# PEER's second choice among 50 sums instead of 256

## The chip, the cores and the metric

The kernel runs on one core of a Trainium2 chip, written in the Tile framework, which puts the instructions of each engine into an order of its own and sets all semaphores. The metric is device time of the whole program in microseconds, as the median of several runs.

## The reference, cut to what matters

Two blocks of a network run over 512 tokens of width 1024: RWKV mixer, feed-forward, gated unit, feed-forward, attention, and at the end PEER, a layer of 16384 one-neuron experts. For each token and each of 8 heads PEER scores two lists of 128 keys, takes the best 16 of each list (first choice), forms all 256 sums of the two lists of sixteen, takes the best 16 of those (second choice), and looks up which pair of keys each winner stands for:

```python
s = jnp.einsum('thpd,hpnd->thpn', q, sub_keys).astype(jnp.float32)
sv, si = lax.top_k(s, PEER_TOPK)
cand = sv[:, :, 0, :, None] + sv[:, :, 1, None, :]
cidx = si[:, :, 0, :, None] * PEER_NKEYS + si[:, :, 1, None, :]
...
fv, fpos = lax.top_k(cand, PEER_TOPK)
eidx = jnp.take_along_axis(cidx, fpos, axis=-1).reshape(C, PEER_HEADS * PEER_TOPK)
g = jax.nn.softmax(fv, axis=-1).reshape(C, PEER_HEADS * PEER_TOPK)
u = u_tab[eidx]
a = jax.nn.gelu(jnp.einsum('ted,td->te', u, hb).astype(jnp.float32), approximate=False)
coef = (g * a).astype(hb.dtype)
vv = v_tab[eidx]
return jnp.einsum('te,ted->td', coef, vv)
```

Both lists come sorted, so a sum at position (a, b) has at least (a+1)(b+1)-1 sums that are no smaller; only pairs with (a+1)(b+1) up to 16 can win, and there are 50 of them.

## The kernel before, in words

The tokens lie in four tiles of 128. Tile 0 gathers its own experts: 256 rows of 1024 numbers are fetched by indirect DMA from GpSimd's queue (L1292) and multiplied on VectorE (L1304, L1308); generator `own`, advanced by `some`. Tiles 1 to 3 do it densely: for each block of 128 experts, an `act` (L1262) multiplies the expert table with all 384 tokens (24 matmuls of 384 columns in three parts; a weight split in two numbers, the high part on ScalarE L102, the low part on VectorE L103, or on GpSimd for every fifth block) and puts the activation into DRAM. 112 of the 128 blocks are computed ahead, as work that `fill` strews among the rest. For tiles 1 to 3 the chosen pairs are turned into weights on a grid of 128 by 128 keys: `onehots` (L1437) makes one-hot rows on VectorE (L1445, L1447, L1450), `grids` (L1453) multiplies them on TensorE (L1470), in 32 units a tile.

The order in which the program is written:

- a loop over 16 half-heads computes the scores; the first choice for tile 0 (`top`, five VectorE operations, L1337 to L1341: max, index of the eight, replace, max, index) stands in it, and an `act` after each fourth;
- `picks(0)`, the second choice and the lookup for tile 0, with `pace(FA, 0)` at each yield; its result `eu`, `ev` (L1435) starts the gathering;
- `tops(1)` to `tops(3)`, the first choice of the other tiles, with half an `act` and 0.3 of an own row a yield;
- `picks(1)`; then `picks(2)` with three units of `grids(1)` a yield, `picks(3)` with those of `grids(2)`, then `grids(3)`;
- `fill(NS)`, the rest of the 112 blocks, and then a loop over 128 blocks that weights the activations and multiplies with the second table; at its 127th step the own rows that are left are done, `some(256)`, and after the last one tile 0 is finished (L1578, L1579) and all are stored.

`picks` yields 14 times: one for each head, one after the softmax, one after the weights are turned, and two for each of two decodings. At each yield `pace` adds 0.2 of an `act` (FB, FA) and, for tiles 1 to 3, 0.2 of an own row (S1). The scheduler takes this order as a priority only: on each engine it picks, by its own estimate of when things are ready, the earliest written instruction that can go, so later work is pulled ahead where an engine would wait. Buffers limit that: the pool of `picks` has two of each tile, the weights three. On the chip each engine then runs its list strictly in order.

A decoding turns 128 positions (0 to 255) into key numbers. For the row a shift, for the column a mask (L1415, L1417); ScalarE widens the 128 numbers to 128 by 16 (L1420), VectorE compares them with 0 to 15 (L1421), multiplies with the sixteen key numbers (L1423) and adds the sixteen up in four steps (L1426, L1428). TensorE then transposes the result (L1399) and ScalarE copies it to `IT` or `JT`, from which `onehots` reads.

Of the kernel before, what the change touches and what calls it, by code (L numbers as in the profile page):

```python
# [9 lines left out]
F32 = mybir.dt.float32  # L10
F32R = mybir.dt.float32r
F16 = mybir.dt.float16
BF = mybir.dt.bfloat16
I32 = mybir.dt.int32
U32 = mybir.dt.uint32
AF = mybir.ActivationFunctionType
OP = mybir.AluOpType
# [23 lines left out]
class Kern:  # L41
# [1193 lines left out]
    def peer(self):  # L1235
        nc, tc, I = self.nc, self.tc, self.I
# [7 lines left out]
        with ExitStack() as cx:  # L1244
# [5 lines left out]
            pi = cy.enter_context(tc.tile_pool(name="pei", bufs=1))  # L1250
            iof = pi.tile([128, 128], F32, name="iof")
            IT, JT = [pi.tile([128, TD], F16, name=n) for n in ("IT", "JT")]
            WW = pi.tile([128, 2, TD], F16, name="WW")
            io4 = pi.tile([128, 128, 4], F16, name="io4")
            io16 = pi.tile([128, 16], F16, name="io16")
# [3 lines left out]
            nc.vector.tensor_copy(io4, iof[:, :, None].to_broadcast([128, 128, 4]))  # L1259
            nc.vector.tensor_copy(io16, iof[:, 0:16])  # L1260

            def act(j, gl=None):  # L1262
                w = self.wload(I["pe_u"][j], [128, 8, 128], eng=nc.gpsimd if j % WP == WP - 1 else None)
                bk = self.bank()[:, 0:TD]
                for k in range(8):
                    self.mm3(bk, (w[0][:, k, :], w[1][:, k, :]), (hT[0][:, k, 128:], hT[1][:, k, 128:]), k == 0, k == 7)
                if gl is None:
                    gl = pg.tile([128, TD], F32, name="gl")
                nc.scalar.activation(gl, bk, AF.Gelu)  # L1269
                return gl  # L1270
# [54 lines left out]
            for h in range(2):  # L1325
                bk = self.bank("x")
# [6 lines left out]
            sv = [pi.tile([128, 16, 16], F32, name=f"sv{t}") for t in range(NT)]  # L1333
            si = [pi.tile([128, 16, 16], U32, name=f"si{t}") for t in range(NT)]

            def top16(src, vals, idx, work):
                nc.vector.max(vals[:, 0:8], src)  # L1337
                nc.vector.max_index(idx[:, 0:8], vals[:, 0:8], src)
                nc.vector.match_replace(work, vals[:, 0:8], src, -3e38)  # L1339
                nc.vector.max(vals[:, 8:16], work)  # L1340
                nc.vector.max_index(idx[:, 8:16], vals[:, 8:16], work)  # L1341
# [8 lines left out]
            with tc.tile_pool(name="pe2", bufs=2) as q2:  # L1350
# [4 lines left out]
                for hp in range(16):  # L1355
# [3 lines left out]
                    bk = self.bank("x")  # L1359
# [15 lines left out]
            def picks(t):  # L1375

                q2 = q3
                fv = q2.tile([128, 8, 16], F32, name="fv")
                fp = q2.tile([128, 8, 16], U32, name="fp")
                for h in range(8):  # L1380
                    cand = q2.tile([128, 256], F32, name="cand")
                    nc.vector.tensor_tensor(cand.rearrange("p (a b) -> p a b", a=16),
                                            sv[t][:, 2 * h, :, None].to_broadcast([128, 16, 16]),
                                            sv[t][:, 2 * h + 1, None, :].to_broadcast([128, 16, 16]), op=OP.add)
                    wk = q2.tile([128, 256], F32, name="wk2")
                    top16(cand, fv[:, h, :], fp[:, h, :], wk)
                    yield
                wt = g0.rearrange("p (h k) -> p h k", h=8) if t == 0 else q2.tile([128, 8, 16], F32, name="wt")
                nc.vector.tensor_tensor(wt, fv, fv[:, :, 0:1].to_broadcast([128, 8, 16]), op=OP.subtract)
                nc.scalar.activation(wt, wt, AF.Exp)  # L1390
# [6 lines left out]
                def turn(src):  # L1397
                    bk = self.bank("x")
                    nc.tensor.transpose(bk[:, 0:128], src.rearrange("p h k -> p (h k)"), self.ident)  # L1399
                    return bk[:, 0:128]  # L1400
# [7 lines left out]
                yield  # L1408
                sif = q2.tile([128, 8, 2, 16], F16, name="sif")
                nc.vector.tensor_copy(sif, si[t].rearrange("p (h e) a -> p h e a", e=2))  # L1410
                ijs = []
                for e, dst in ((0, IT), (1, JT)):
                    ab = q2.tile([128, 8, 16], U32, name="ab")
                    if e == 0:
                        nc.vector.tensor_scalar(ab, fp, 4, None, op0=OP.logical_shift_right)  # L1415
                    else:
                        nc.vector.tensor_scalar(ab, fp, 15, None, op0=OP.bitwise_and)  # L1417
                    oh = q2.tile([128, 8, 16, 16], F16, name="oh")
                    ohr = oh.rearrange("p h k a -> p (h k) a")
                    nc.scalar.copy(ohr, ab.rearrange("p h k -> p (h k)")[:, :, None].to_broadcast([128, 128, 16]))  # L1420
                    nc.vector.tensor_tensor(ohr, ohr, io16[:, None, :].to_broadcast([128, 128, 16]), op=OP.is_equal)  # L1421
                    yield
                    nc.vector.tensor_mul(oh, oh, sif[:, :, e, None, :].to_broadcast([128, 8, 16, 16]))  # L1423

                    for n in (8, 4, 2):
                        nc.vector.tensor_add(ohr[:, :, 0:n], ohr[:, :, 0:n], ohr[:, :, n:2 * n])  # L1426
                    ij = q2.tile([128, 8, 16], F32, name="ij")
                    nc.vector.tensor_add(ij.rearrange("p h k -> p (h k)"), ohr[:, :, 0], ohr[:, :, 1])  # L1428
                    yield
                    if t:  # L1430
                        nc.scalar.copy(dst[:, ts], turn(ij))
                    ijs.append(ij.rearrange("p h k -> p (h k)"))
                if t == 0:
                    for dst, m, n in ((eu, ijs[0], ijs[1]), (ev, ijs[1], ijs[0])):
                        nc.vector.scalar_tensor_tensor(dst, m, 128.0, n, op0=OP.mult, op1=OP.add)  # L1435
# [246 lines left out]
```

## Time and profile before

| | us |
|---|---|
| median of 3 runs | 3099.87 (3099.35 to 3113.97) |
| profiled execution, its own time | 3095.69 |
| its span | 3093.9 |
| TensorE busy | 2951.7 (95%) |
| VectorE busy | 2091.1 (68%) |
| ScalarE busy | 1156.3 (37%) |
| GpSimd busy | 646.3 (21%) |
| mean granted TensorE clock | 0.971 |

The span is from the first instruction to the last; the execution's own time has 1.8 us more around it. Busy time says little by itself: matmuls overlap, so a busy TensorE is judged by how many it starts in a stretch. Operations of VectorE overlap too: the duration of a row is longer than the distance to the next row's start, and it is that distance that the engine's time goes by. PEER begins at about 1756 us and holds the last 43% of the span.

### The profile page before, as it was taken

What the parts mean: (1) busy time and instruction counts of PE and PEld (TensorE: products, weight loads), DVE (VectorE), ACT (ScalarE), POOL (GpSimd) and SP (SyncE); (2) the same over time, 40 slices, a digit from 0 to 9 for tenths busy, and PEclk for the clock granted to TensorE, in tenths of its full rate; (3) what the DMA queues carried; (4) which work ended last, traced back from release to release, by engine and by line L of the source; (5) the groups of instructions that cost most, each with busy time, mean ns of one, the idle gap of its engine ahead of it and who ended that gap; (6) DMA issues with size and microseconds to landing.
All of it is one profiled execution on the core that took longest, in us unless ns stands there. A gap on an engine that the chain in (4) does not pass through costs nothing.

```text
span 3093.9 us, 43610 instructions
## 1 busy us (share of the span) xinstructions
PE 2951.7 (95%) x16121; PEld 2483.1 (80%) x16121; DVE 2091.1 (68%) x4694; ACT 1156.3 (37%) x1918; POOL 646.3 (21%) x593
## 2 busy tenths in 40 slices
PE   7977899999999999999999999989999999999998
PEld 6755787888888788888875888989999888787887
DVE  7663775533247666425776678999988477888787
ACT  5533433322223332223565433344433333333332
POOL 1023221000000000000000003345444434444453
PEclk9978999999999999999998999999999999999999
DMA  4235654222324267533220234678888889999996
GB/s 143 92 85 192 162 144 130 93 91 95 95 89 143 76 214 234 164 95 92 77 85 2 68 101 161 227 244 294 282 292 287 294 307 322 336 341 321 327 335 223
DMA packets 217553, 569.03 MB, mean 184 GB/s; under 512 B 64474, under 2 KB 80090, under 8 KB 217212
## 3 DMA queue, kind: packets, MB, share of 16 engines
q1 hardware_dynamic: 144508, 362.71, 35.8%
q0 software_dynamic: 64096, 200.89, 19.1%
q10 hardware_dynamic: 8736, 2.65, 0.4%
q8 instruction: 126, 2.06, 0.3%
q14 instruction: 87, 0.71, 0.1%
HBM read 504.24 MB, written 61.87 MB: 183 GB/s over the span
## 4 chain that ended last, share of the span: by engine, by line
PE 75%; DVE 12%; DMA 6%; issue 4%; ACT 2%; POOL 1%; POOLq 0%; SPq 0%; DVEq 0%; ACTq 0%
PE b L276 19%; PE b L124 15%; PE b L123 15%; PE b L122 15%; PE b L1470 3%; DMA gl<-ga 2%; DVE wlo L103 2%; DVE er L1304 1%; PE b L1161 1%; PE b L959 1%; DVE hr L1308 1%; DMA er<-in_pe_ur,eu 1%; PE b L1179 1%; DVE wk L1339 1%; PE b L678 1%
## 5 line engine op out<-in xcount | busy, mean ns | idle before, releaser
L102 ACT CAST whi<-wst 128x1024 fp32r<-128x1024 f32 (+2 forms) x491 | 510.7, 1041 | 1165.4 <-PE b L123 436.1
L103 DVE TENSOR_TENSOR wlo<-wst,whi 128x1024 fp32r<-128x1024 f32 (+2 forms) x466 | 563.3, 1210 | 442.5 <-ACT whi L102 426.2
L124 PE MATMUL b<-hTh,wlo 128*128 128x384 f32 (+2 forms) x1992 | 716.4, 360 | 13.7 <-DVE wlo L103 13.4
L122 PE MATMUL b<-hTh,whi 128*128 128x384 f32 (+2 forms) x1992 | 722.4, 363 | 2.5 <-ACT hTh L223 1.5
L123 PE MATMUL b<-hTl,whi 128*128 128x384 f32 (+2 forms) x1992 | 717.0, 360 | 2.2 <-DVE hTl L224 2.2
L124 PEld LDWEIGHTS b<-hTh,wlo 128*128 128x128 f32 x1992 | 377.7, 190 | 57.0 <-DVE wlo L103 18.4
L122 PEld LDWEIGHTS b<-hTh,whi 128*128 128x128 f32 x1992 | 379.2, 191 | 42.3 <-ACT hTh L223 2.2
L123 PEld LDWEIGHTS b<-hTl,whi 128*128 128x128 f32 x1992 | 378.4, 190 | 40.9 <-DVE hTl L224 3.0
L122 PE MATMUL b<-whi,ch 128*128 128x512 f32 x768 | 304.7, 397 | 5.4 <-ACT ch L102 5.4
L124 PE MATMUL b<-whi,cl 128*128 128x512 f32 x768 | 304.6, 397 | 1.2 <-DVE cl L103 1.2
L123 PE MATMUL b<-wlo,ch 128*128 128x512 f32 x768 | 304.5, 396 | 0.3 <-DVE wlo L103 0.3
L1292 POOL DMA_INDIRECT er<-in_pe_v,ev x128 | 196.0, 1531 | 241.1 <-DVE hr L1308 216.1
L1292 POOL DMA_INDIRECT er<-in_pe_ur,eu x128 | 171.6, 1340 | 90.1 <-DVE er L1304 58.5
L122 PEld LDWEIGHTS b<-whi,ch 128*128 128x128 f32 x768 | 144.8, 189 | 39.8 <-ACT ch L102 5.7
L124 PEld LDWEIGHTS b<-whi,cl 128*128 128x128 f32 x768 | 144.6, 188 | 36.8 <-DVE cl L103 2.0
L123 PEld LDWEIGHTS b<-wlo,ch 128*128 128x128 f32 x768 | 144.8, 189 | 34.9 <-DVE wlo L103 0.7
L1308 DVE SCALAR_TENSOR_TENSOR hr<-er,a,hr 128x1024 f32<-128x1024 f32 x127 | 164.4, 1294 | 0.1
L1304 DVE SCALAR_TENSOR_TENSOR er<-er,hr 128x1024 f32<-128x1024 f32 x128 | 156.3, 1225 | 8.5 <-DMA er<-in_pe_ur,eu 8.5
L1274 POOL DMA_DIRECT2D ga<-gl x112 | 64.8, 579 | 345.1 <-ACT gl L1269 332.0
L276 PE MATMUL b<-whi,hTh 128*128 128x512 f32 (+2 forms) x336 | 129.3, 386 | 0.8 <-ACT P L971 0.8
L276 PE MATMUL b<-whi,hTl 128*128 128x512 f32 (+2 forms) x336 | 129.4, 385 | 0.4 <-DVE hTl L103 0.4
L276 PE MATMUL b<-wlo,hTh 128*128 128x512 f32 (+2 forms) x336 | 129.6, 386 | 0.0
(556 smaller groups left out, 4954.8 us busy)
## 6 DMA issues: line engine op xcount, KB each, us to landing
wst<-in_pe_u SPq DMA_DIRECT2D x128, 512.0 KB, 4.7
wst<-in_pe_v SPq DMA_DIRECT2D x128, 512.0 KB, 6.2
wst<-in_ffn_gu SPq DMA_DIRECT2D x88, 512.0 KB, 3.7
wst<-in_ad_w SPq DMA_DIRECT2D x48, 512.0 KB, 4.1
wst<-in_ffn_dn SPq DMA_DIRECT2D x44, 512.0 KB, 3.6
ga<-gl POOLq DMA_DIRECT2D x112, 192.0 KB, 4.2
gl<-ga SPq DMA_DIRECT2D x112, 192.0 KB, 5.0
gd<-G SPq DMA_DIRECT2D x40, 512.0 KB, 6.5
```

Source lines behind the costliest of these rows:

```text
L102: self.nc.scalar.copy(hi, src)
L103: (eng or self.nc.vector).tensor_sub(lo, src, hi)
L122: mm(out, a[0], b[0], start=start, stop=False)
L123: mm(out, a[0], b[1], start=False, stop=False)
L124: mm(out, a[1], b[0], start=False, stop=stop)
L276: self.nc.tensor.matmul(banks[t][:, :n], self.chunk(aT, a, k + kk)[:, t * 128:(t + 1) * 128], w[b][:, kk, :], start=seen[t] == 1, stop=see ...
L678: mm(bk[:, q * 256:(q + 1) * 256], BT[:, c, 2 * g + q, :], AT[:, c, 2 * g + q].rearrange("p e n -> p (e n)"), start=True, stop=True)
L1274: nc.gpsimd.dma_start(ga[j], act(j))
L1292: d = nc.gpsimd.indirect_dma_start(out=r, out_offset=None, in_=src, in_offset=bass.IndirectOffsetOnAxis(ap=idx[:, k:k + 1], axis=0))
L1304: d = nc.vector.scalar_tensor_tensor(r, r, 1.0, hr, op0=OP.mult, op1=OP.mult, accum_out=a0[:, k:k + 1])
L1308: d = nc.vector.scalar_tensor_tensor(y0, r, a0[:, k - 128:k - 127], y0, op0=OP.mult, op1=OP.add)
L1470: mm(bk[:, e * 128:(e + 1) * 128], oi[:, u % OT // 4, :, e], oj[:, w, u % OT // 4, :, e], start=(w == 0), stop=(w == 1))
```

## The change

The sums of all eight heads are formed at once, and only the 50 that can win: seven additions (rows a = 0, 1, 2, 3, 4 with 16, 8, 5, 4 and 3 sums each, rows 5 to 7 together with 2 each, rows 8 to 15 together with 1 each) replace eight of 256. So the second choice of any head stands behind the first choice of all heads. The five operations of the choice run on 50 elements; `picks` yields once after the sums, once for each two heads, once each after the softmax and the weights, and five times in the lookup: 12 times in place of 14.

A position 0 to 49 no longer holds row and column in its bits. The position is compared with the sixteen starts of the rows (`st16`): the result is 1 for each row up to the right one. Multiplied with the differences between neighbouring key numbers (`dsi`) and added up, that is the row's key number; multiplied with the row lengths (`dst16`) and added up, it is the row's start, which is taken from the position to give the column, and the column is decoded as before. So there are three sums over sixteen in place of two, and the second widening waits for the first. Two constants are made once, with 18 small fills on GpSimd.

```diff
--- before.py
+++ after.py
@@ -1259,6 +1259,18 @@
             nc.vector.tensor_copy(io4, iof[:, :, None].to_broadcast([128, 128, 4]))
             nc.vector.tensor_copy(io16, iof[:, 0:16])
 
+
+            NC = 50
+            seg = [16, 8, 5, 4, 3, 2, 2, 2] + [1] * 8
+            begin = [sum(seg[:a]) for a in range(16)]
+            st16, dst16 = [pi.tile([128, 16], F16, name=n) for n in ("st16", "dst16")]
+            nc.vector.tensor_scalar(st16, iof[:, 0:16], 34.0, None, op0=OP.add)
+            for a in range(8):
+                nc.gpsimd.memset(st16[:, a:a + 1], float(begin[a]))
+            nc.gpsimd.memset(dst16, 1.0)
+            for a in range(9):
+                nc.gpsimd.memset(dst16[:, a:a + 1], float(seg[a - 1]) if a else 0.0)
+
             def act(j, gl=None):
                 w = self.wload(I["pe_u"][j], [128, 8, 128], eng=nc.gpsimd if j % WP == WP - 1 else None)
                 bk = self.bank()[:, 0:TD]
@@ -1377,14 +1389,26 @@
                 q2 = q3
                 fv = q2.tile([128, 8, 16], F32, name="fv")
                 fp = q2.tile([128, 8, 16], U32, name="fp")
+                cand = q2.tile([128, 8, NC], F32, name="cand")
+                s2 = sv[t].rearrange("p (h e) k -> p h e k", e=2)
+                for a0_, a1_ in ((0, 1), (1, 2), (2, 3), (3, 4), (4, 5), (5, 8), (8, 16)):
+                    m, n = a1_ - a0_, seg[a0_]
+                    o = cand[:, :, begin[a0_]:begin[a0_] + m * n]
+                    sa, sb = s2[:, :, 0, a0_:a1_], s2[:, :, 1, 0:n]
+                    if m == 1:
+                        nc.vector.tensor_tensor(o, sb, sa.to_broadcast([128, 8, n]), op=OP.add)
+                    elif n == 1:
+                        nc.vector.tensor_tensor(o, sa, sb.to_broadcast([128, 8, m]), op=OP.add)
+                    else:
+                        nc.vector.tensor_tensor(o.rearrange("p h (a b) -> p h a b", a=m),
+                                                sa[:, :, :, None].to_broadcast([128, 8, m, n]),
+                                                sb[:, :, None, :].to_broadcast([128, 8, m, n]), op=OP.add)
+                yield
                 for h in range(8):
-                    cand = q2.tile([128, 256], F32, name="cand")
-                    nc.vector.tensor_tensor(cand.rearrange("p (a b) -> p a b", a=16),
-                                            sv[t][:, 2 * h, :, None].to_broadcast([128, 16, 16]),
-                                            sv[t][:, 2 * h + 1, None, :].to_broadcast([128, 16, 16]), op=OP.add)
-                    wk = q2.tile([128, 256], F32, name="wk2")
-                    top16(cand, fv[:, h, :], fp[:, h, :], wk)
-                    yield
+                    wk = q2.tile([128, NC], F32, name="wk2")
+                    top16(cand[:, h, :], fv[:, h, :], fp[:, h, :], wk)
+                    if h % 2:
+                        yield
                 wt = g0.rearrange("p (h k) -> p h k", h=8) if t == 0 else q2.tile([128, 8, 16], F32, name="wt")
                 nc.vector.tensor_tensor(wt, fv, fv[:, :, 0:1].to_broadcast([128, 8, 16]), op=OP.subtract)
                 nc.scalar.activation(wt, wt, AF.Exp)
@@ -1408,28 +1432,56 @@
                 yield
                 sif = q2.tile([128, 8, 2, 16], F16, name="sif")
                 nc.vector.tensor_copy(sif, si[t].rearrange("p (h e) a -> p h e a", e=2))
+                fpf = q2.tile([128, 128], F16, name="fpf")
+                nc.vector.tensor_copy(fpf, fp.rearrange("p h k -> p (h k)"))
+                dsi = q2.tile([128, 8, 16], F16, name="dsi")
+                nc.vector.tensor_copy(dsi[:, :, 0:1], sif[:, :, 0, 0:1])
+                nc.vector.tensor_sub(dsi[:, :, 1:16], sif[:, :, 0, 1:16], sif[:, :, 0, 0:15])
+                sh = [128, 128, 16]
                 ijs = []
-                for e, dst in ((0, IT), (1, JT)):
-                    ab = q2.tile([128, 8, 16], U32, name="ab")
-                    if e == 0:
-                        nc.vector.tensor_scalar(ab, fp, 4, None, op0=OP.logical_shift_right)
-                    else:
-                        nc.vector.tensor_scalar(ab, fp, 15, None, op0=OP.bitwise_and)
-                    oh = q2.tile([128, 8, 16, 16], F16, name="oh")
-                    ohr = oh.rearrange("p h k a -> p (h k) a")
-                    nc.scalar.copy(ohr, ab.rearrange("p h k -> p (h k)")[:, :, None].to_broadcast([128, 128, 16]))
-                    nc.vector.tensor_tensor(ohr, ohr, io16[:, None, :].to_broadcast([128, 128, 16]), op=OP.is_equal)
-                    yield
-                    nc.vector.tensor_mul(oh, oh, sif[:, :, e, None, :].to_broadcast([128, 8, 16, 16]))
-
+
+                def wide(src):
+                    oh = q2.tile(sh, F16, name="oh")
+                    nc.scalar.copy(oh, src[:, :, None].to_broadcast(sh))
+                    return oh
+
+                def total(oh, out):
                     for n in (8, 4, 2):
-                        nc.vector.tensor_add(ohr[:, :, 0:n], ohr[:, :, 0:n], ohr[:, :, n:2 * n])
-                    ij = q2.tile([128, 8, 16], F32, name="ij")
-                    nc.vector.tensor_add(ij.rearrange("p h k -> p (h k)"), ohr[:, :, 0], ohr[:, :, 1])
-                    yield
+                        nc.vector.tensor_add(oh[:, :, 0:n], oh[:, :, 0:n], oh[:, :, n:2 * n])
+                    nc.vector.tensor_add(out, oh[:, :, 0], oh[:, :, 1])
+
+                def numbers(oh, row):
+                    o4 = oh.rearrange("p (h k) a -> p h k a", h=8)
+                    nc.vector.tensor_mul(o4, o4, row[:, :, None, :].to_broadcast([128, 8, 16, 16]))
+                    ij = q2.tile([128, 128], F32, name="ij")
+                    total(oh, ij)
+                    return ij
+
+                def turned(ij, dst):
                     if t:
-                        nc.scalar.copy(dst[:, ts], turn(ij))
-                    ijs.append(ij.rearrange("p h k -> p (h k)"))
+                        bk = self.bank("x")
+                        nc.tensor.transpose(bk[:, 0:128], ij, self.ident)
+                        nc.scalar.copy(dst[:, ts], bk[:, 0:128])
+                    ijs.append(ij)
+
+                oh = wide(fpf)
+                nc.vector.tensor_tensor(oh, oh, st16[:, None, :].to_broadcast(sh), op=OP.is_ge)
+                yield
+                o2 = q2.tile(sh, F16, name="oh")
+                nc.vector.tensor_mul(o2, oh, dst16[:, None, :].to_broadcast(sh))
+                bg = q2.tile([128, 128], F16, name="bg")
+                total(o2, bg)
+                nc.vector.tensor_sub(fpf, fpf, bg)
+                yield
+                ij = numbers(oh, dsi)
+                yield
+                turned(ij, IT)
+                oh = wide(fpf)
+                nc.vector.tensor_tensor(oh, oh, io16[:, None, :].to_broadcast(sh), op=OP.is_equal)
+                yield
+                ij = numbers(oh, sif[:, :, 1, :])
+                yield
+                turned(ij, JT)
                 if t == 0:
                     for dst, m, n in ((eu, ijs[0], ijs[1]), (ev, ijs[1], ijs[0])):
                         nc.vector.scalar_tensor_tensor(dst, m, 128.0, n, op0=OP.mult, op1=OP.add)
```

## Rows read from the trace of the kernel before

**Rows 1.** Windows by stage: length, busy us (xcount) by engine, clock, DMA, GB/s.

```profile
1784.00:1890.00 106.00, 106.00 (x542) 89.95 (x541) 79.00 (x358) 40.52 (x98) 4.60 (x5) 1.00 0.28 94
...
1890.00:1908.00 18.00, 12.75 (x67) 12.05 (x66) 18.00 (x70) 9.46 (x10) 8.60 (x4) 0.85 0.24 85
1908.00:1950.00 42.00, 42.00 (x237) 42.00 (x236) 38.05 (x169) 14.01 (x20) 23.13 (x21) 0.98 0.83 285
1950.00:1985.00 35.00, 33.27 (x184) 31.70 (x184) 35.00 (x132) 10.46 (x16) 14.49 (x15) 1.00 0.71 237
1985.00:2050.00 65.00, 54.05 (x306) 50.59 (x305) 63.67 (x159) 28.16 (x39) 22.59 (x22) 0.95 0.61 205
...
2130.00:2170.00 40.00, 35.30 (x221) 33.99 (x221) 34.84 (x91) 12.95 (x23) 20.48 (x19) 0.98 0.91 318
2170.00:2265.00 95.00, 95.00 (x593) 91.73 (x593) 92.07 (x189) 43.51 (x63) 42.91 (x38) 0.97 0.79 272
```

**Rows 2.** Waits of TensorE, 1780 to 2500 us: total us, times, longest.

```profile
PE b L1470 <- DVE oj L1450: 11.6, 2, 6.9
PE b L124 <- DVE wlo L103: 10.0, 6, 4.5
```

**Rows 3.** Timeline of TensorE (start, duration, idle before): gaps and matmul spacing.

```profile
1906.05 0.69 PE L124 MATMUL b<-hTh,wlo 128*128 128x384 f32 x1 [4.45 <-DVE wlo L103]
...
1908.45 0.52 PE L122 MATMUL b<-hTh,whi 128*128 128x384 f32 x1
1908.78 0.52 PE L123 MATMUL b<-hTl,whi 128*128 128x384 f32 x1
...
2035.63 0.28 PE L1470 MATMUL b<-oj,oi 128*128 128x128 f16 x1 [6.92 <-DVE oj L1450]
...
2160.69 0.38 PE L1399 MATMUL b<-ident,ij 128*128 128x128 f32 x2
...
2169.41 0.30 PE L1470 MATMUL b<-oj,oi 128*128 128x128 f16 x1 [4.70 <-DVE oj L1450]
```

**Rows 4.** VectorE's groups by line and form, 1780 to 1890 us.

```profile
L1382 DVE TENSOR_TENSOR cand<-sv 128x256 f32<-128x256 f32 x8 | 3.3, 406 | 0.0
```

**Rows 5.** VectorE's groups by line and form, 1960 to 2050 us.

```profile
L1382 DVE TENSOR_TENSOR cand<-sv 128x256 f32<-128x256 f32 x16 | 7.5, 476 | 0.0
```

**Rows 6.** Timeline of VectorE: second choice of one head, sum to sum.

```profile
2163.65 0.41 DVE L1382 TENSOR_TENSOR cand<-sv 128x256 f32<-128x256 f32 x1
...
2165.82 0.41 DVE L1382 TENSOR_TENSOR cand<-sv 128x256 f32<-128x256 f32 x1
2166.15 0.41 DVE L1340 MAX8 fv<-wk 128x8 f32<-128x256 f32 x1
```

**Rows 7.** Timeline of VectorE: operations on 8 and on 128 elements.

```profile
1893.44 0.18 DVE L1393 RECIPROCAL wsum<-wsum 128x8 f32<-128x8 f32 x1
1893.54 0.25 DVE L1340 MAX8 sv<-wk 128x8 f32<-128x128 f32 x1
...
1914.01 0.27 DVE L1340 MAX8 sv<-wk 128x8 f32<-128x128 f32 x1
1914.20 0.07 DVE L1339 MATCH_VALUE_LOAD wk<-sv,sc 128x8 f32 x1
```

**Rows 8.** Timeline of VectorE: tile 0's first row of one-hots summed.

```profile
1900.87 0.70 DVE L1426 TENSOR_TENSOR oh<-oh 128x1024 f16<-128x1024 f16 x1
1901.47 1.23 DVE L1423 TENSOR_TENSOR oh<-oh,sif 128x2048 f16<-128x2048 f16 x1
1902.60 1.66 DVE L1426 TENSOR_TENSOR oh<-oh 128x512 f16<-128x512 f16 x4
```

**Rows 9.** Timeline of GpSimd beside that decoding.

```profile
1901.02 9.06 POOL L103 TENSOR_TENSOR wlo<-wst,whi 128x1024 fp32r<-128x1024 f32 x1 [0.18 <-ACT whi L102]
```

**Rows 10.** Line L103 on GpSimd: duration ns min/median/max, first and last start.

```profile
L103 POOL TENSOR_TENSOR wlo<-wst,whi x25: 2372/2572/9062, 1876.3 to 2948.5; 128x1024 fp32r<-128x1024 f32 x25
```

**Rows 11.** Timeline of VectorE at the end: the last own row.

```profile
3076.71 1.27 DVE L1308 SCALAR_TENSOR_TENSOR hr<-er,a,hr 128x1024 f32<-128x1024 f32 x1
```


## The prediction

> **What bounds the kernel now.** I read the shares of busy time first, then the windows by stage, the waits of TensorE, the timeline of its gaps and last the timeline of VectorE. By the shares in the table TensorE is the bound, 95% busy. By stages that holds except in one stretch of PEER. From 1784 to 1890 us, where the scores and tile 0's first choice are made, TensorE is never idle and VectorE has 16 us to spare in 106. From 1890 to 2050 VectorE is full (18.0 of 18, 38.1 of 42, 35.0 of 35, 63.7 of 65) and TensorE is not (12.8, 42, 33.3, 54.1). From 2050 on TensorE is full again, but for a hole before 2170 [rows 1]. TensorE's waits in PEER name VectorE: 11.6 us for the grids' one-hot rows, in two gaps, and 10.0 us for low parts of weights, in six [rows 2]. The gaps stand at 1906 (4.5), 2035.6 (6.9) and 2169.4 (4.7) [rows 3]; the other five low-part gaps come to 5.5. So this part of PEER can give at most these 21.6 us and what the clock loses behind them. The change works on the engine that causes them.
>
> **What goes.** A head's second choice takes VectorE 2.17 us from one sum to the next [rows 6], eight heads of a tile 17.4. But tile 0's eight sums all start before 1890 [rows 4], where TensorE is the bound and VectorE has time over: of their 17.4 us I count 2.2, the last head's, as exposed.
>
> **What comes, the choice.** On 50 elements an operation is not in the trace. By distance of starts one of 8 elements takes 0.10 us, one of 128 takes 0.19 [rows 7], one of 256 takes 0.33 [rows 6]; so 50 lies between 0.10 and 0.19, and I take 0.12, by the slope from 128 to 256 and a little over. Five operations and three loads of 0.06 [rows 7] make 0.8 a head, 6.4 a tile. Seven additions of 24 to 128 sums at 0.13 make 0.9. Sum 7.3 us a tile; from 5.5+0.8 = 6.3 (all at 0.10) to 9.1+1.4 = 10.5 (0.19 for the choice, 0.2 for additions). If they are chains that wait for each other, which two heads in turn should hide, the duration of 0.27 [rows 7] would count in place of the distance and a tile would cost 12 to 14.
>
> [...]
>
> **What comes, the lookup.** A third sum over sixteen: a multiplication of 2048 at 1.13, then additions at 0.60, and four more steps over 1.57 us in pairs from two chains, 0.3 to 0.4 each, so 1.6 for a chain [rows 8]. A cast, a subtraction and two differences, four small operations at 0.1 to 0.2, against two shifts of the same size: +0.4. So 3.1 us a tile more, between 2.6 and 3.6. The comparisons and widenings stay two, but the second widening now waits for the first sum: this chain is longer by some 4 us a tile and shows only where the lookup is waited for.
>
> **By stages.** Tile 0 stands bare behind its last first choice: 7.3 + 3.1 - 2.2 = +8.2. Tile 1: 7.3 + 3.1 - 17.4 = -7.0. Tile 2's heads are done before the first grid too, in VectorE's list ahead of the one-hot rows (16 sums start between 1960 and 2050, tile 1's and 2's [rows 5]): 7.3 - 17.4 = -10.1. The 12 yields for 14 shift the strewn work: adding up `pace`, 32 blocks instead of 33 lie ahead of the first grid and 16 own rows instead of 17, so VectorE loses a split (1.1) and a row (1.2 to 1.3). Sum -11.2. From the ends above -15 to -1; with 13 a tile it is +6. VectorE starts the one-hot rows ahead of 2035.6 accordingly, at 2024.4. TensorE without the one block (24 matmuls of 0.177 [rows 1] = 4.2 us) is through its list at 2028.7 - 4.2 = 2024.5, if its small gaps stay. So the first grid starts at about 2025, 10.6 earlier; but the block left out has to be done later, where TensorE is the bound. Net -6.4 (with +6 on VectorE: +10; with -15: -7, or -10 with the small gaps shut).
>
> Tile 3: six of its heads (13 us) stand in VectorE's list ahead of tile 2's one-hot rows, the last one's sum at 2165.8 [rows 6], after the transposition at 2160.7 that the one-hot rows need [rows 3]. The 7.3 us in their place can be over before it. The gap of 4.7 shrinks to about 1, the distance from the transposition through ScalarE to the first product: -3.7, from 0 to -4.7.
>
> [...] Two gaps gone: -2.5, from 0 to -4. Tile 3's lookup falls where VectorE has 3 us free in 95 [rows 1]: +0.5 (0 to 3). At the end the own rows count 250 instead of 251 before the remainder, so one more follows in the chain of the last ones, which then decides the end: +1.2 [rows 11], from 0 to 1.3. The 18 fills and one small operation for the constants stand at 1756, GpSimd having been idle for long: 0. In all two blocks move to `fill(NS)`; the second leaves a stretch where TensorE is full and comes back in one, so only the 4.2 above count.
>
> Sum: -6.4 - 3.7 - 2.5 + 0.5 + 1.2 = -10.9. The profiled execution took 3095.7 of its own; the median of the runs is 4.2 higher. 3099.9 - 10.9 = **3089**.
>
> **Rivals.**
> *All gaps close.* VectorE's relief also shuts the small gaps and the first one: of 21.6 us some 3 stay, and the clock's 4 come back: -18.6 - 4 + 1.7 = -21, 3079. For it: every one of these gaps ends on VectorE [rows 2]. Against: at 1900 to 1906 VectorE gets more to do, not less.
>
> *Nothing is won.* The one-hot rows also wait for the column's numbers, and their transposition stands at the end of TensorE's list for the tile, as at 2160.7 [rows 3]. With the longer chain the gaps at 2035 and 2169 stay, with another cause. Then +0.5 + 1.2, and 0 to -2 from small gaps: 3100.
>
> *Slower: tile 0 loses its cover.* At 1901 TensorE is out of low parts already. If the scheduler puts all 7.3 + 3.1 us more ahead of the splits, being written earlier, the gap of 4.5 there grows by 10 to 13. Up to 1950 TensorE is the bound (42 of 42 [rows 1]), so it isn't won back; the first grid then starts when TensorE is through its blocks, at 2037, and one block is owed: +6. With the gap at 2169 kept and the end's +1.2: +7 to +9, 3108. Gains elsewhere come to 11, so it decides from a growth of 11 us at that gap. Against it: the split needed there takes 1.1 us, and the longer chain leaves VectorE pauses of two widenings.
>
> *GpSimd is blocked.* Beside tile 0's lookup one split on GpSimd took 9.06 us [rows 9], against 2.57 in the median [rows 10]. With 2.7 us more of VectorE's work in the lookup the split lasts 12, and if TensorE wants the block two of 4.2 us after the split began, it waits 3 to 4 us and the first gathers, queued behind it, too: 3093. [...]
>
> **How the numbers follow.** Forecast 0.44 (by itself 3083 to 3096), all gaps 0.21, nothing won 0.17, slower 0.12, GpSimd 0.06. Half a per cent, 15.5 us, is about what a measurement of this kernel can tell from no change: faster means below 3084.4, slower above 3115.4. All gaps lies nearly whole below (0.18) and a quarter of the forecast, its lower end (0.11): faster 0.29. Above lie only the slower case's upper end and a list ordered otherwise than thought: 0.09. Same 0.62. The range, 3076 to 3104, takes in all gaps but its best end and half of the slower case.
>
> **What would show it.** Right: L1337 to L1341 on 50 elements at distances of 0.11 to 0.13; 17 us a tile down to 7; VectorE's first L1445 at 2022 to 2028 and the wait for L1450 down from 11.6 us to under 4; one more L1308 at the end. Wrong: distances near 0.2; the gap at 1901 above 10 us; the gaps at the grids' starts kept with the transposition or ScalarE as the last cause; other stages moved.

## The result, and the profile after

The kernel after takes 3124.91 us in the median, the kernel before 3104.04 in the runs beside it: ratio 1.0073, 95% interval 1.0059 to 1.0086. The forecast was 3089, with a range that ended at 3104: it is slower, by some 22 us, where a gain of 11 was forecast.

The profiled execution of after, the fastest of its twenty, has a span of 3107.4, 13.5 more than that of before. Its time can't be compared stage by stage on the clock of the profile: the last product of the scores, up to which TensorE has the same work in both kernels, starts at 1883.24 in before and at 1869.90 in after. Over all the profiles of this case it lies between 1869.9 and 1887.9, with the old choice as with the new one. So every stage below is counted from that product. Then the time from it to the end is 13.5 + 13.3 = 26.9 us longer (before rounding): 6.1 up to the first product of the loop over 128 blocks, 19.3 in that loop, 1.5 behind its last product.

| from the last score product, us | first grid | loop starts | loop lasts | behind it |
|---|---|---|---|---|
| before | 152.4 | 586.8 | 614.3 | 9.5 |
| after | 149.0 | 592.9 | 633.6 | 11.0 |

The stages of [rows 1] in after, moved by those 13.3 us (length, then busy us and count of TensorE, weight loads, VectorE, ScalarE and GpSimd, granted clock, DMA share, GB/s):

```profile
1876.66:1894.66 18.00, 14.58 (x83) 13.94 (x81) 18.00 (x79) 10.61 (x11) 6.88 (x4) 1.00 0.31 96
1894.66:1936.66 42.00, 37.60 (x192) 36.64 (x193) 39.56 (x136) 12.34 (x18) 19.23 (x20) 0.92 0.78 273
1936.66:1971.66 35.00, 35.00 (x200) 35.00 (x200) 35.00 (x178) 12.10 (x17) 15.99 (x15) 1.00 0.78 237
1971.66:2036.66 65.00, 56.53 (x308) 53.44 (x307) 60.06 (x200) 29.63 (x40) 41.41 (x21) 0.92 0.52 164
2116.66:2156.66 40.00, 38.16 (x240) 36.88 (x238) 38.32 (x74) 21.86 (x30) 16.97 (x15) 1.00 0.83 282
2156.66:2251.66 95.00, 94.94 (x605) 92.22 (x606) 85.51 (x163) 37.23 (x61) 48.32 (x39) 1.00 0.84 292
```

VectorE is still full, or nearly, up to the first grid; only in the last of these stages has it 9.5 us free in 95 where it had 3 [rows 1]. TensorE's gaps there have moved more than they have closed. The first group is what it waited for from 1767 to 2460 (us, times, longest), against [rows 2]; the second its timeline, against [rows 3]:

```profile
PE b L1522 <- DVE oj L1502: 9.0, 3, 3.9
PE b L124 <- DVE wlo L103: 7.9, 4, 3.2
PE b L124 <- POOL wlo L103: 3.3, 2, 3.1
```

```profile
1895.24 0.44 PE L124 MATMUL b<-hTh,wlo 128*128 128x384 f32 x1 [3.13 <-POOL wlo L103]
...
1983.73 0.69 PE L124 MATMUL b<-hTh,wlo 128*128 128x384 f32 x1 [3.20 <-DVE wlo L103]
...
2018.92 0.27 PE L1522 MATMUL b<-oj,oi 128*128 128x128 f16 x1 [3.85 <-DVE oj L1502]
...
2110.53 1.32 PE L1522 MATMUL b<-oj,oi 128*128 128x128 f16 x8 [3.28 <-DVE oj L1502]
...
2156.72 0.29 PE L1522 MATMUL b<-oj,oi 128*128 128x128 f16 x1 [1.90 <-DVE oj L1502]
```

The choice itself got as short as forecast. In VectorE's timeline a head's second choice now goes from 1877.53 to 1878.31, 0.78 us, against 2.17 [rows 6]:

```profile
1877.53 0.20 DVE L1349 MAX8 fv<-cand 128x8 f32<-128x50 f32 x1
1877.64 0.21 DVE L1352 MAX8 fv<-wk 128x8 f32<-128x50 f32 x1
1877.77 0.08 DVE L1350 MATCH_VALUE_LOAD fp<-fv,cand 128x8 f32 x1
1877.84 0.20 DVE L1350 FIND_INDEX8 fp<-fv,cand 128x8 uint32<-128x50 f32 x1
...
1878.31 0.21 DVE L1349 MAX8 fv<-cand 128x8 f32<-128x50 f32 x1
```

An operation on 50 elements lasts 0.20 us and the next starts after 0.11 to 0.13.

The loop is the larger part. Its window in before, from its first product to its last, and the same in after:

```profile
2470.06:3084.37 614.31, 609.33 (x2695) 501.96 (x2696) 501.31 (x845) 209.36 (x287) 262.28 (x185) 1.00 0.91 317
```

```profile
2462.80:3096.42 633.62, 617.04 (x2696) 505.02 (x2696) 503.21 (x847) 210.49 (x287) 260.28 (x185) 0.99 0.88 306
```

The work is the same (2695 or 2696 matmuls, 185 operations of GpSimd); in before the loop is TensorE's to 99%, in after TensorE is idle for 16.6 us. In before it is idle there for 5.0, so 11.6 of the 19.3 us are idle time; the other 7.7 are the same products taking longer, 617.0 for 609.3, at a mean granted clock of 0.99 in place of 1.00. In after TensorE waits in the loop for low parts that VectorE makes:

```profile
PE b L123 <- DVE wlo L103: 8.2, 8, 2.5
PE b L124 <- DVE wlo L103: 5.1, 2, 3.6
```

In before those two rows are 0.3 and 3.4. Nothing in the loop's code is changed.

### The profile page after: what moved, and what is told of

The parts are those of the page before. It is cut to its first block, busy times and chain, and to the rows that moved or that the text cites. A ratio compares the mean times of both kernels' runs of the same rounds, so it can differ in the third digit from the quotient of the medians.

```text
span 3107.4 us, 43669 instructions
## 1 busy us (share of the span) xinstructions
PE 2944.8 (95%) x16121; PEld 2477.6 (80%) x16121; DVE 2063.6 (66%) x4719; ACT 1157.2 (37%) x1918; POOL 654.7 (21%) x611
## 4 chain that ended last, share of the span: by engine, by line
PE 58%; DVE 16%; DMA 14%; issue 7%; ACT 3%; POOL 1%; DVEq 0%; POOLq 0%; SPq 0%; ACTq 0%
PE b L276 19%; PE b L124 10%; PE b L123 10%; PE b L122 10%; DMA gl<-ga 5%; DVE wlo L103 3%; PE b L1522 2%; DMA wst<-in_ad_w 2%; DVE hr L1320 2%; DMA wst<-in_ffn_gu 1%; DMA wst<-in_pe_v 1%; DMA er<-in_pe_ur,eu 1%; DVE er L1316 1%; ACT whi L102 1%; DVE cl L103 1%
## 5 line engine op out<-in xcount | busy, mean ns | idle before, releaser
L103 DVE TENSOR_TENSOR wlo<-wst,whi 128x1024 fp32r<-128x1024 f32 (+2 forms) x466 | 567.6, 1219 | 455.2 <-ACT whi L102 440.4
L124 PE MATMUL b<-hTh,wlo 128*128 128x384 f32 (+2 forms) x1992 | 719.6, 361 | 18.6 <-DVE wlo L103 14.1
L124 PEld LDWEIGHTS b<-hTh,wlo 128*128 128x128 f32 x1992 | 379.5, 191 | 62.2 <-DVE wlo L103 18.6
L1304 POOL DMA_INDIRECT er<-in_pe_ur,eu x128 | 185.4, 1448 | 94.7 <-DVE er L1316 54.7
L123 PEld LDWEIGHTS b<-wlo,ch 128*128 128x128 f32 x768 | 145.7, 190 | 47.2 <-DVE wlo L103 13.3
```

What stands on the lines that cost most here:

```text
L103: (eng or self.nc.vector).tensor_sub(lo, src, hi)
L123: mm(out, a[0], b[1], start=False, stop=False)
L124: mm(out, a[1], b[0], start=False, stop=stop)
L1304: d = nc.gpsimd.indirect_dma_start(out=r, out_offset=None, in_=src, in_offset=bass.IndirectOffsetOnAxis(ap=idx[:, k:k + 1], axis=0))
```

## The experiments

Each was timed in five rounds beside the kernel before; ratios are to before, with 95% intervals. Stage times are of one profile each, counted as in the table; the loop's differ by up to 12 us between kernels that have the same fraction of a row owed at its start.

**The pacing or the choice?** Two things changed without being meant: with 12 yields in place of 14 fewer blocks and fewer own rows are strewn ahead. *e1* is after with both scaled up again:

```diff
-FA, FT, FB, FG, FL = .2, .5, .2, .6508, .7484
-S0, S1, S2, SL, S3 = .3, .2, .7, .8, 1.2492
+FA, FT, FB, FG, FL = .2 * 14 / 12, .5, .2 * 14 / 12, .6508, .7484
+S0, S1, S2, SL, S3 = .3, .2 * 14 / 12, .7, .8, 1.2492
```

> The changed kernel, with FA, FB and S1 times 14/12, so that its 12 yields strew as many blocks and own rows as the 14 did (104 blocks and 93 rows before the second loop). Theory (pace): the change itself wins about 7 to 10 us up to the second loop, and the 20 us lost in that loop come from the own rows being at another place in their count of 1.2492 a step, which reorders the loop's lists. Then the loop takes 612 to 618 us again and the whole is 0.996 to 0.998 of before. Rival (the choice itself: the earlier, changed lists upset the loop whatever the count): the loop stays at 630 to 638, the whole at 1.006 to 1.008.

Measured 0.9998 (0.9984 to 1.0013), the loop 625.9. With before's pacing the loss is gone, but the gain that this theory left to the choice isn't there either: by the interval it is worth at most 5 us. *e2* gives before the fewer own rows of after, with no part of the choice (`S1` times 12/14; by adding up, 92.0 rows are owed at the loop's start in place of 93.2, so it is one row fewer, and another fraction):

> The kernel before, with S1 alone times 12/14: two own rows fewer are done before the second loop, nothing else. Theory (pace): the loop gets slower by 15 to 22 us, the whole 1.005 to 1.008 of before, though no part of the second choice is changed. Rival (the choice itself): 0.999 to 1.001. Rival (the two blocks that moved to the end): 0.999 to 1.001.

Measured 1.0064 (1.0047 to 1.008), the loop 639.8: nearly all of the loss, without the change. *e3* gives before the fewer blocks (`FA` and `FB` times 12/14):

> The kernel before, with FA and FB alone times 12/14: two blocks fewer are done before the end of the grids and two more in one piece ahead of the second loop. Theory (pace of the own rows): the loop is untouched, the whole 0.998 to 1.002. Rival (the blocks that moved): 1.005 to 1.008.

Measured 0.9977 (0.9963 to 0.9992), a little faster. It beats both kernels. So it is the own rows. (Before with both scaled down at once wasn't run.) By adding up `pace`, 93.2 are owed at the loop's start in before and 92.0 in after. *e4* is after with the count begun higher, which leaves 92 rows done but restores the fraction:

```diff
-            due = [0.0]
+            due = [0.2]
```

> The changed kernel, with the own rows' count started at 0.2 instead of 0: at the second loop the count stands at 92.2 where the kernel before has 93.2 and the changed one 92.0, so the fraction is that of before and the number of rows nearly that of the changed kernel. Theory (the fraction decides which of four steps takes two rows, and so the loop's lists): the loop takes 612 to 618 us, the whole 0.996 to 0.999 of before. Rival (the number of rows or blocks left over): the loop stays at 630 to 638, the whole at 1.005 to 1.008.

Measured 0.9995 (0.9979 to 1.0011); the loop 625.5, 8 less than in after though not the 612 to 618 expected, the end behind it still 11.0. The converse is *e5*, before with `due = [-0.2]`, 93 rows done and nothing over:

> The kernel before with one number changed: the running count of owed own rows starts at -0.2, so the loop over 128 blocks begins with 93 rows done as before, but with a fraction of 0.0 owed in place of 0.2. Theory A (the fraction decides at which blocks two rows fall due, and so the order in which the loop's loads stand in SP's queue): about 3122, ratio 1.006 to 1.008, the loop from its first to its last matmul some 635 us in place of 614 to 626. Rival B (it is the number of rows that are left for the loop, one more): no change, ratio 0.999 to 1.001.

Measured 1.0032 (1.0011 to 1.0054), the loop 637.4, the end 9.6: the loop is as long as theory A had it, the whole slower by half of what it gave. So the number of rows (rival B) is not what costs; the fraction is. A step of the loop owes 1.2492 rows, so one step in four does two, and the fraction sets which one.

**The parts.** *e8* and *e9* have before's 14 yields, so blocks and rows stand as in before. *e8* replaces only the choice:

```diff
+                for a0_, a1_ in ((0, 1), (1, 2), (2, 3), (3, 4), (4, 5), (5, 8), (8, 16)):
...
                 for h in range(8):
-                    cand = q2.tile([128, 256], F32, name="cand")
...
-                    wk = q2.tile([128, 256], F32, name="wk2")
-                    top16(cand, fv[:, h, :], fp[:, h, :], wk)
+                    wk = q2.tile([128, NC], F32, name="wk2")
+                    top16(cand[:, h, :], fv[:, h, :], fp[:, h, :], wk)
                     yield
```

> The kernel before with the choice alone: seven additions for all heads and five operations on 50 elements a head, but with before's yield for each head and before's decoding, which takes wrong experts (the positions 0 to 49 are read as if they were 0 to 255). Blocks and own rows stand where they stand in before. My prediction's terms: 17.4 to 7.3 us a tile, the first grid about 16 us earlier with no block owed, less the lookup's part: by them 3082 to 3088, ratio 0.994 to 0.996. Rival E (VectorE's list takes later work forward into the time won, and TensorE has its other gaps): 3092 to 3099, ratio 0.9975 to 1.0.

Measured 0.9987 (0.9964 to 1.001); the first grid at 157.3, which is later than in before, the loop at 586.2. Rival E fits, and the lists show how. Operations of VectorE from the last score product to its first one-hot rows for a grid, before first, then *e8* (busy us, mean ns):

```profile
L1421 DVE TENSOR_TENSOR oh<-oh,io 128x2048 f16<-128x2048 f16 x4 | 7.6, 1888 | 0.0
L1340 DVE MAX8 fv<-wk 128x8 f32<-128x256 f32 x17 | 7.0, 414 | 0.0
```

```profile
L1435 DVE TENSOR_TENSOR oh<-oh,io 128x2048 f16<-128x2048 f16 x6 | 9.7, 1613 | 0.0
L1344 DVE MAX8 fv<-wk 128x8 f32<-128x50 f32 x32 | 6.6, 205 | 0.0
```

Two comparisons make a tile's lookup and eight of these MAX8 its choice. Before has two lookups and two choices (and one head) ahead of the one-hot rows; *e8* has three lookups and four choices. What the shorter choice sets free is taken up by tile 2's lookup and tile 3's choice, which stood behind the one-hot rows before, and by seven heads of tile 0, which stood ahead of the last score product. *e9* keeps before's choice and takes after's decoding, of which one yield is left out:

```diff
                 nc.vector.tensor_sub(fpf, fpf, bg)
-                yield
                 ij = numbers(oh, dsi)
```

> The kernel before with the new lookup alone: before's choice among 256 sums and its yields, and after's three sums over sixteen with one yield fewer, so that a tile has 14 yields as before. It takes wrong columns, as positions run to 255. Blocks and own rows stand where before has them. By the terms of the prediction 3.1 us a tile more on VectorE: the first grid 7 us later (it counts the tiles 0 and 1, and part of 2), the time 3106 to 3110, ratio 1.002 to 1.0035. Rival E (VectorE's list closes up elsewhere): 3100 to 3104, ratio 0.9995 to 1.001.

Measured 1.0002 (0.9986 to 1.0019), the first grid at 151.0, the loop at 587.2. The reverse of *e8*: more work a tile costs nothing that shows either, as less of the choice now stands ahead of the grid (119 operations of it after the last score product, 155 in before). *e15* is after with the own rows scaled (`S1` times 14/12) and the blocks as in after:

> The kernel after with own rows alone scaled by 14/12 at a yield of the choice, so that the loop begins with 93.2 rows as in before; the blocks stay as in after. By the runs so far: as the kernel with the count starting at 0.2 (0.9995), less 1.5 us at the end for the row that is no longer late, 3094 to 3099, ratio 0.998 to 1.000. If the choice had the worth that I predicted (10.9 us): 3088 to 3092, ratio 0.9955 to 0.997.

Measured 1.0011 (0.9995 to 1.0026), the loop at 584.2 and 620.9 long. It has the blocks and rows of *e3* and the choice of after, and is slower than *e3* (0.9977), with intervals that don't overlap: with after's blocks the choice doesn't gain, but seems to cost some 10 us. Their two profiles differ by only 1 us from the last score product on, so where these 10 us lie isn't shown.

**Why another order costs in the loop.** My theory A was that on SP's queue loads of activations (L1616), waiting for a free buffer, now stand ahead of loads of weights. *e6* takes them from that queue, *e7* is the control, *e4* with the same edit:

```diff
-                    nc.sync.dma_start(gl, ga[j])
+                    nc.scalar.dma_start(gl, ga[j])
```

> The kernel after, but in the loop over 128 blocks the load of a block's activations is issued from ScalarE's queue in place of SP's. VectorE's, GpSimd's and TensorE's lists stay those of after. Theory A (weight loads stand behind activation loads that wait for a buffer, on SP's queue): the 20 us go, 3095 to 3105, ratio 0.997 to 1.001. Rival C (the cost is in VectorE's list, where a pair of own rows now stands ahead of a split or a product): about as after, 3115 to 3125, ratio 1.004 to 1.008. Rival D (ScalarE's high parts and roundings now stand behind the waiting loads): slower than after, above 3130.

> The control of the run before: the kernel after with the count of owed rows starting at 0.2 (which by itself ran at 0.9995 of before), and the activations' loads on ScalarE's queue. Theory A: the same time as the run before, within 0.2%. Rival C: 20 us faster than the run before. Rival D: as slow as the run before, both above 3130.

Measured 1.0106 (1.0072 to 1.014) and 1.0021 (0.9997 to 1.0044); the loops 640.6 and 629.9. The move costs 8 to 10 us in both, and the difference between the two orders is as it was: that the order costs by way of SP's queue has fallen. Of the three named there VectorE's list is left (rival C). Its timeline in after, and TensorE's beside it:

```profile
2846.15 0.49 DVE L1618 TENSOR_TENSOR gl<-gl,gte 128x320 f32<-128x320 f32 x1 [4.16 <-DMA gl<-ga]
2846.61 1.28 DVE L1320 SCALAR_TENSOR_TENSOR hr<-er,a,hr 128x1024 f32<-128x1024 f32 x1
2847.82 1.22 DVE L103 TENSOR_TENSOR wlo<-wst,whi 128x1024 fp32r<-128x1024 f32 x1
```

```profile
2844.93 0.34 PE L122 MATMUL b<-hTh,whi 128*128 128x384 f32 x1
2845.10 0.34 PE L123 MATMUL b<-hTl,whi 128*128 128x384 f32 x1
2849.09 0.48 PE L124 MATMUL b<-hTh,wlo 128*128 128x384 f32 x1 [3.65 <-DVE wlo L103]
```

TensorE has the high part of the weight at 2844.93. The split for the low part stands behind a product with an activation whose load hasn't landed, for which VectorE stands still for 4.16 us, and behind an own row; TensorE loses 3.65. Which step has two rows would then matter by where it lies to the late blocks' splits (theory G). *e10* and *e11* are after with `due` at 0.45 and 0.7, which puts the two rows into the other two steps of four:

> The kernel after with the count of owed own rows starting at 0.45: in the loop over 128 blocks the step that does two own rows is then the one with number 2 of every four, where it was number 0 in after and number 3 in before (0.2). A block that was not computed ahead has its weights split in every eighth step, two steps ahead of its use, in a step with number 1. Theory G (two rows cost where they fall in or just ahead of that step, as VectorE's list then has an activation's product that waits for its load ahead of the split): as good as 0.2, 3097 to 3103, ratio 0.9985 to 1.0005, the loop 620 to 627. Theory H (any order other than that for which before was tuned costs): 3112 to 3125, the loop above 633.

> The same with 0.7: the two rows fall into the step with number 1, where the late block's weights are split. Theory G: slow, 3115 to 3128, ratio 1.004 to 1.008, the loop above 633. Theory H: slow as well. If both this and the run before are fast, it is number 0 alone that costs.

Measured 1.0136 (1.0109 to 1.0163) and 1.0033 (1.0016 to 1.0049), the loops 656.1 and 632.5. Theory G has fallen: the step that it held to be good is the worst. Three of the four orders are slower than the one that before has. What grows with the loop is VectorE's wait for activations. The window of the loop in *e10*, then the waits of VectorE in it:

```profile
2466.20:3122.30 656.10, 623.85 (x2695) 508.03 (x2696) 503.99 (x845) 208.88 (x287) 253.16 (x185) 0.98 0.87 297
```

```profile
DVE gl L1618 <- DMA gl<-ga: 125.7, 66, 5.4
DVE wlo L103 <- ACT whi L102: 24.0, 22, 3.0
```

The first of these rows is 78.4 us (44 times) in the loop of before (614.3 long), 82.6 (42) in *e3* (621.9), 89.9 (46) in *e4* (625.5), 93.3 (47) in after (633.6). That they go together doesn't yet show which causes which, and over all the profiles the tie is loose: 89.4 in *e9* (615.7), 94.8 in *e1* (625.9). TensorE's waits for low parts from VectorE (both rows added up) order the loops better: 3.7 us in before, 4.3 in *e9*, 7.5 in *e3*, 11.3 in *e4*, 11.7 in *e1*, 13.3 in after, 18.6 in *e2* (639.8), 29.1 in *e10*. *e12* has one more buffer for the activations, `PG` 5 in place of 4, in after:

> The kernel after with five buffers for a block's activations in place of four, the owed rows unchanged (number 0 of four). If VectorE's waits for the activations' loads (87 us in the loop's trace of after, 72 in before) hold the splits up, because a load can't be issued until a buffer is free: the loop falls from 634 to 620 to 627, the time to 3100 to 3110, ratio 1.000 to 1.003. If the waits only show that the loop's DMAs are full: no change, 3118 to 3126, ratio 1.006 to 1.008.

(Over the whole loop these waits are 93.3 and 78.4 us, not 87 and 72.) Measured 1.0075 (1.0051 to 1.0099), the loop 629.6: buffers don't help. *e13* takes some of the transfers away, *e14* is the control from *e4*:

```diff
-                if j % GR == 0:
-                    gt = q2.tile([128, CD - KG, GR, CT], F32, name="gte" if j < NS else "gtl", bufs=GB if j < NS else 2)
+                if j % GR == 0 and (j >= GR and j < NS or j >= NS + GR):
+                    gts[j // GR] = gts[0 if j < NS else NS // GR]
+                elif j % GR == 0:
+                    gt = q2.tile([128, CD - KG, GR, CT], F32, name="gte" if j < NS else "gtl", bufs=1)
```

> The kernel after with the grid's weights (tile gte) loaded once in place of once for every four blocks: 27 loads of 655 KB fewer in the loop, some 9% of what its DMAs move; the outputs of tiles 1 to 3 are then wrong. The lists of VectorE, ScalarE, TensorE and SP in the loop stay those of after. Theory J (another order of VectorE's list costs because the DMAs are nearly full and the loads of the activations land late): the loop falls from 634 to 612 to 620, VectorE's waits for those loads from 87 to under 60 us, and the kernel comes within 0.3% of the next run. Rival K (the order costs by itself, whatever the DMAs carry): the loop stays above 628, and the kernel 0.6 to 0.9% slower than the next run.

> The control: the same in the kernel after with the owed rows starting at 0.2 (0.9995 of before by itself, its loop 625.5). Theory J: the loop 612 to 618, the time 0.2 to 0.5% under before. Rival K: the loop 615 to 625.

Measured 0.9978 (0.9959 to 0.9997) and 0.9955 (0.9936 to 0.9975). The loop of *e13*, what VectorE waits for in it, and all that TensorE waits for in it:

```profile
2469.66:3080.19 610.53, 608.32 (x2696) 502.69 (x2696) 505.39 (x847) 209.14 (x287) 228.95 (x158) 0.99 0.84 289
```

```profile
DVE gl L1620 <- DMA gl<-ga: 58.4, 43, 3.5
```

```profile
PE b L122 <- ACT ch L102: 8.5, 1, 8.5
PE b L124 <- DVE cl L103: 2.2, 1, 2.2
```

With 27 loads fewer the order of after takes 610.5 us, that of *e4* 611.7, and TensorE waits for no low part in the order of after. So the loop is as theory J had it: after's order costs only together with these loads. That it is by the load on the DMAs is argued, not shown. For it: the only loads for which VectorE waits in the loop are those of activations (`gl<-ga`), of SP's queue, 93.3 us in after and 58.4 in *e13*. But the loads that were taken away are issued from GpSimd's queue, and no run tells that queue from the bytes. Nor was the like run made with the orders of *e10* and *e11*; in *e10* the activations land as soon after their issue as in before (5.0 and 4.9 us in the median, 5.6 in after), so there at least they are not slow to come.

The two kernels still differ by 0.23%, with intervals that overlap. In their profiles a difference is left ahead of the loop: it starts at 593.9 in *e13* and at 584.1 in *e14*, as at 592.9 in after and 586.7 in *e4*, and at 594.2 in *e6* and 587.5 in *e7*.

## Why the prediction was wrong, step by step

*The own rows: the step that failed most.* The prediction worked out that 250 of them stand ahead of the remainder in place of 251, and priced that with one row at the end, +1.2. That row came (11.0 behind the loop for 9.5). But the running count also sets the order of the loop's lists, and there it cost 15 us: the loop lasts 614.3 to 625.9 in the seven kernels with before's fraction and before's queue (before, *e1*, *e3*, *e4*, *e8*, *e9*, *e15*; mean 621.4), and 633.6 to 639.8 in after, *e2* and *e5* (mean 636.9). Ahead of the loop it cost some 6 more, 592.9 for 586.7 in *e4*: the loop's first product waits 8.7 us in after (5.8 in *e4*), and a gap of 3.28 at 2110.53 is new. That part goes with the new choice: before with the same fraction starts its loop at 588.1 (*e2*) and 585.5 (*e5*), where before has 586.8. Why the order costs in the loop is open beyond what *e13* and *e14* show. I had listed "a list ordered otherwise than thought" with no price at all.

*The choice, 17.4 to 7.3 us a tile: right.* 0.78 to 0.80 a head was forecast as 0.8. *The lookup, +3.1 a tile: about right*, 3.5 by *e9*.

*A reading of [rows 1]* was wrong: from 1784 to 1890 VectorE has 27 us to spare (79.00 busy in 106.00); the 16 are what the weight loads leave (89.95). The price of tile 0's choice, 2.2, doesn't change by it.

*VectorE starts the one-hot rows 11.2 us earlier: wrong.* From the last score product to them VectorE's time by distances of starts fell from 150.4 to 147.0 only. The choice gave 38.8 - 22.6 = 16.2; the lookups took 32.5 - 18.6 = 13.9 of it where 6.2 was reckoned, as the first half of tile 2's lookup now stands ahead too, and one sum of sixteen beside a split on GpSimd took 2.66 us. I had taken the list of before, and put shorter operations into it.

*First grid 10.6 earlier, net -6.4: wrong*, 3.4 earlier with the same block owed, net +0.8. *The gap at the second grid, -3.7:* it shrank from 4.70 to 1.90, but the new one at 2110.53 is 3.28. *The clock, -2.5: wrong, it took time.* No run shows the -2.5, nor what one gap costs by the clock; the runs show the granted clock in the 4 us behind each of TensorE's gaps over 3 us between the scores and the loop, a mean of 0.60, 0.58 and 0.50 in before (gaps of 4.45, 6.92 and 4.70) and of 0.72, 0.50, 0.62 and 0.50 in after (3.13, 3.20, 3.85 and 3.28), and 1.00 behind the gap of 1.90. The stages above have 1.00 where before has 0.85, but 0.92 in two places where before has 0.98 and 0.95. From the last score product to the loop's first the mean is 0.98 in before and 0.97 in after, and as many products keep TensorE busy for 562.7 us in place of 558.8 (before first, columns as above):

```profile
1883.24:2470.06 586.82, 558.84 (x3393) 540.23 (x3392) 508.25 (x1234) 235.81 (x351) 269.12 (x237) 0.98 0.78 267
1869.90:2462.80 592.90, 562.68 (x3394) 545.71 (x3393) 494.80 (x1316) 235.59 (x351) 277.65 (x236) 0.97 0.77 265
```

*The choice as a whole* is worth nothing that *e1* (0.9998), *e8* (0.9987) and *e9* (1.0002) could show, not 10.9 us. TensorE's gaps over 0.4 us from the last score product to the loop's first come to 27.5 us in before, 22.3 in *e1* and 22.6 in *e8*: at the grids they shrink from 11.6 to 3.5 and 1.4, at the low parts they grow from 9.7 to 13.6 in both, and the loop starts only 1.9 and 0.7 us earlier.

*The rivals.* "Nothing is won" has the sum of the choice, though not its way: in *e1* and *e8* the gaps at the grids didn't stay. "Slower" has the sign, but not the place: the gap beside tile 0's lookup didn't grow (3.13 for 4.45). "GpSimd is blocked" came in part, in place of the gap at 1906: TensorE waits 3.13 us for the split beside tile 0's lookup, as that rival had it, but the split takes 5.78 us, less than the 9.06 of before and not 12. None of the rivals had the loop in it.

## What to carry to other kernels

Where generators strew work by running fractions, a change in the number of yields is a change of every list behind it, far from the code that was edited: compare those lists before pricing anything, and keep the count. Time freed on an engine whose order a scheduler makes can go to other work that is ready, as in *e8*, and not to the operation that was late. This loop, at 0.99 of TensorE and 0.9 of the DMAs, took badly to another order: of the four that were tried, the three that before doesn't have made the kernel slower by 10 to 42 us.

## What the runs showed of the hardware

In two places of after a split on GpSimd and a sum on VectorE beside it both took longer. GpSimd's rows, then VectorE's:

```profile
1889.41 5.78 POOL L103 TENSOR_TENSOR wlo<-wst,whi 128x1024 fp32r<-128x1024 f32 x1
...
1991.38 4.72 POOL L103 TENSOR_TENSOR wlo<-wst,whi 128x1024 fp32r<-128x1024 f32 x1 [4.57 <-ACT whi L102]
```

```profile
1993.55 0.28 DVE L1474 TENSOR_TENSOR fpf<-fpf,bg 128x128 f16<-128x128 f16 x1
1993.74 2.66 DVE L1451 TENSOR_TENSOR ij<-oh 128x128 f32<-128x128 f16 x1
1996.33 0.19 DVE L1352 MAX8 fv<-wk 128x8 f32<-128x50 f32 x1
```

The second split takes 4.72 us, against 2.43 in the median of the 25 in after and 2.57 in that of before [rows 10], and a sum of 128 numbers 2.66, against 0.46 in the median of the eight in after; it ends 0.3 after the split, which ends at 1996.1. It is the same at 1889.41: there the sum takes 2.53 us and ends 0.25 after the split. In both places the sum starts 2.3 to 2.4 us ahead of the split's end, about as long as a split takes in the median. Operations of two inputs that start in the split ahead of the sum keep near their times: that at 1993.55 takes 0.28, where such an operation takes 0.21 to 0.28 in the four tiles. Nor does every split last longer: 22 of the 25 take 2.38 to 2.64 us. What held the two splits and the two sums up isn't shown.
